# One transformer layer with product-key experts: all first expert products before the second ones, the second product with its operands exchanged, routing weights by accumulating scatters

## The chip, the cores and the metric

The kernel runs on one core of one Trainium2 chip. The metric is the device time of one execution in microseconds, the median of three runs. Five engines matter: PE (TensorE matmul, with PEld for its weight loads), DVE (VectorE), ACT (ScalarE), POOL (GpSimd, which also issues the indirect transfers) and SP (SyncE, which issues most loads). Matrix work is fp32: each operand is split in a high and a low half, and each 128-row block takes three products, hi·hi, hi·lo and lo·hi.

## The reference

256 prompt tokens and 64 sample tokens pass one layer of width 2048: attention in three branches, gates, an output product, and then a layer of 16,384 experts, which takes most of the time:

```python
s = jnp.einsum('thpc,hpkc->thpk', q, sub_keys)          # 8 heads, 2 halves, 128 keys
s1, i1 = lax.top_k(s[:, :, 0], 16); s2, i2 = lax.top_k(s[:, :, 1], 16)
cand_s = s1[..., :, None] + s2[..., None, :]
top_s, top_j = lax.top_k(cand_s.reshape(tb, 8, 256), 16)
eidx = take(i1 * 128 + i2, top_j); g = softmax(top_s)   # 128 experts per token
a = gelu(einsum('td,thkd->thk', xb, expert_u[eidx]))
return einsum('thk,thkd->td', g * a, expert_v[eidx])
```

## The kernel before, in words

One program holds all instructions; a planner with estimated clocks (`Plan`) writes out the order in which they stand on each engine. Weight matrices come as tiles of 512 KB ("halves"): SP loads `raw` (128x1024), ACT writes `hi`, DVE writes `lo` = raw - hi, and PE does the 24 matmuls of the half (`Stream`, L359; every other operation is recorded by one helper, L221). Each engine runs its instructions in order: a DVE instruction that waits holds up every `lo` behind it.

The first 1,129 us are the attention part and the query product. Then come the experts. For the 256 prompt tokens every expert is computed densely, in 32 groups of 4x128 experts:

- `Up(e)`: x times `pu`, two halves of 24 matmuls 128x256 (the tile is the stationary operand, 256 tokens move). ACT applies gelu and writes `hs`. Groups below `NSPILL` = 20 are written to memory (`hd`) and read back later.
- `weigh`: `hs` times the routing weights `gg` (zero for experts not chosen) gives `w`, split in hi and lo.
- `Down(q, c)`: `w` times `pv`, summed in PSUM over 8x128 experts, added by DVE to `x2` (the sum `r<-r,mm`, features by tokens). 256 tokens move.
- The order is 22 groups of Up (NSPILL + RES), then Up and Down alternately, then Down alone.

The routing weights G are built by `g_unit`, 64 units of four tokens: DVE makes one-hot tiles `ob` and `oa` of the chosen keys, POOL multiplies `ob` with the high and the low half of the weights (`wH`, `wL`), PE multiplies `oa` and `ob` (four matmuls `bk`), ACT and DVE put both halves together in `st`, and SP writes it to memory as `gd`, which is read back as `gg`.

The 64 sample tokens are not computed densely. For each of two tables (`pur`, `pvr`), 128 indirect gathers on POOL fetch 128 rows of 4 KB into one of four `gs` slots. DVE takes a product with a running sum of each `pur` tile (`dot`, form `gs<-gs,xs`), and adds each `pvr` tile times a weight to `x2s` (`axpy`). The next gather into a slot waits for the DVE instruction that reads it.

The few lines behind this that the steps below touch (`split_one` of the stream, `dot`, and the operands of Up and of Down, stationary or moving by their place):

```python
            act.activation(hi, raw, AF.Copy)
            dve.tensor_tensor(lo, raw, hi, op=ALU.subtract)
...
        plan.see(gs)
        yield
        dve.scalar_tensor_tensor(gs, gs, 1.0, R["xs"], op0=ALU.mult, op1=ALU.mult, accum_out=R["dots"][:, j:j + 1])
        X["GS"].give(gs)
...
            w, e = w_of[self.q], b % 8
            return self.ps[:, :DN], w[:, 0, e, :], w[:, 1, e, :], e == 0, e == 7
```

Of the kernel before, what the change touches and what calls it, by code (L numbers as in the profile page):

```python
# [33 lines left out]
RES = 2  # L34
NSPILL = 20
NGS = 4
HSN = 4
RATE = 380e3
GLAT = 5.0
# [3 lines left out]
TB = 16  # L43
LA = 5
SA = 3

# [34 lines left out]

class Task:
# [4 lines left out]
class Plan:  # L87
# [4 lines left out]
    def __init__(self):  # L92
        self.clk = {e: 0.0 for e in ("pe", "act", "dve", "pool", "dma")}
        self.task = self.main = Task(None)
        self.tasks = []
        self.done = {}
        self.uses = {}
        self.table = None

# [37 lines left out]
    def move(self, queue, out, src):  # L137

        at = max(self.last(out, True), self.last(src, False))
        if queue != "sync":  # L140
            at = self.clk[queue] = max(self.clk[queue], at) + (1.0 if queue == "pool" else 0.1)
        n = size(out) * out.shape[0] * 4
        self.clk["dma"] = max(self.clk["dma"], at) + n / RATE
        self.touch(out, self.clk["dma"] + 2.0, True)
        self.touch(src, self.clk["dma"] + 2.0, False)

    def gather(self, out, idx):
        at = self.clk["pool"] = max(self.clk["pool"], self.last(out, True), self.last(idx, False)) + 1.05
        self.clk["dma"] = max(self.clk["dma"], at) + size(out) * out.shape[0] * 4 / RATE
        self.touch(out, self.clk["dma"] + GLAT, True)  # L150

# [5 lines left out]
    def spawn(self, gen):  # L157
        self.tasks.append(Task(gen, self.task.at))
# [53 lines left out]
class Engine:  # L212
# [4 lines left out]
    def __getattr__(self, op):  # L217
        f = getattr(self.eng, op)

        def call(*a, **k):  # L220
# [4 lines left out]
            if op == "indirect_dma_start":  # L225
                p.gather(out, k["in_offset"].ap)
                return r
# [13 lines left out]
def pe_cost(op, a, k):  # L241
    n = size(a[2]) / (2.4e3 if op == "matmul" and a[2].dtype == F32R else 0.6e3)
    return max(0.107, n + 0.003) if op == "matmul" else 0.216
# [6 lines left out]
def dve_cost(op, a, k):  # L250
# [3 lines left out]
    return 0.07 + n / 0.96e3 * (6.2 if op == "reciprocal" else 1)  # L254
# [12 lines left out]
def hybrid_kernel(ctx: ExitStack, tc: tile.TileContext, ins, outs, stop=None):  # L267
# [20 lines left out]
    RAW = Slots(plan, stream, "raw", [128, 1024], F32, LA)  # L288
    HI = Slots(plan, stream, "hi", [128, 1024], F32R, SA + 1)
    LO = Slots(plan, stream, "lo", [128, 1024], F32R, SA + 1)  # L290
# [11 lines left out]
    pool.memset(one, 1.0)  # L302
    mhalf = consts.tile([128, 1], F32, name="mhalf")
# [5 lines left out]
    class Stream:  # L309
        def __init__(self):  # L310
            self.loads, self.halves = deque(), deque()

        def fetch(self):
            p, h = next(self.src, (None, 0))
            if p is None:
                return False
            raw = RAW.take()
            p.load(raw, h)
            self.loads.append((p, h, raw))
            return True  # L320

        def split_one(self):
            p, h, raw = self.loads.popleft()
            hi, lo = HI.take(), LO.take()
            act.activation(hi, raw, AF.Copy)
            dve.tensor_tensor(lo, raw, hi, op=ALU.subtract)
            RAW.give(raw)
            self.halves.append((p, h, hi, lo))

        def fill(self):  # L330
            while RAW.free and self.fetch():
                pass

        def ahead(self):
            self.fill()
            while HI.free and self.loads:
                if self.halves and plan.last(self.loads[0][2], False) > plan.now() + 1:
# [10 lines left out]
        def half(self):  # L348
            p, h, hi, lo = self.halves.popleft()
# [17 lines left out]
            HI.give(hi)  # L367
            LO.give(lo)

    eng = Stream()  # L370

    class Piece:

        GAP = 0.0025
# [135 lines left out]

    s1 = ExitStack()
# [24 lines left out]
    def late_consts():  # L536
# [17 lines left out]
        dve.tensor_scalar(bgh, vec[:, V_BG:V_BG + 48], 0.5, None, op0=ALU.mult)  # L554

# [442 lines left out]
    spawn(late_consts())  # L998

# [131 lines left out]
    def open_route():  # L1131
# [3 lines left out]
        R["x2s"], R["xs"] = (p.tile([128, W], F32, name=n) for n in ("x2s", "xs"))  # L1135
        p = open_pool(route, "route")
        for n in ("iT0", "iT1", "wH", "wL"):
            R[n] = p.tile([128, DN], F32R if n == "wH" else F32, name=n)
        for n in ("idx", "wS", "dots", "act"):
            R[n] = p.tile([128, 128], U32 if n == "idx" else F32, name=n)  # L1140
# [13 lines left out]
        spawn(rows_task())  # L1154
        for _ in range(LANES):
            spawn(route_lane())
        spawn(weights_lane())
# [19 lines left out]
    def rows_task():  # L1177

        x2s, xs = R["x2s"], R["xs"]
        for a in range(PARTS):  # L1180
            pool.dma_start(xs[a * S:a * S + S], ins["gffn"][a:a + 1].to_broadcast([S, W]))
        yield from need(("xb",))
        for k0 in range(0, KT, 4):
            bk, = yield from take(BK)
            a = k0 * 128 // W
            n, rows, c = S * a + S, slice(S * a, S * a + S), k0 * 128 % W
            for k in range(4):
                pe.transpose(bk[:n, k * 128:k * 128 + 128], x2[:, k0 + k, T - n:T], ident)
            yield
            act.activation(x2s[rows, c:c + 512], bk[rows, :], AF.Copy)  # L1190
            BK.give(bk)
# [5 lines left out]
        dve.scalar_tensor_tensor(xs, x2s, r2[:, 3:4], xs, op0=ALU.mult, op1=ALU.mult)  # L1197

# [4 lines left out]
    def wq_in(h, p):  # L1203
        def go(ps):
# [9 lines left out]
            if p == 1:  # L1214
                plan.see(sk)
                yield
                for i in range(3):
# [66 lines left out]
    def weights_lane():  # L1284
        yield from need(*[("dec", i) for i in range(3)])
        rtmp.close()
        q = open_pool(gtmp, "gtmp")
        OA = Slots(plan, q, "oa", [128, 4, 128], F32R, 3)
        OB = Slots(plan, q, "ob", [128, 4, 2, 128], F32R, 3)
        ST = Slots(plan, q, "st", [128, 128, TB], F32, 2)  # L1290
        st = None
        for t0 in range(0, DN, 4):
            if t0 % TB == 0:
                st, = yield from take(ST)
            oa, ob = yield from take(OA, OB)
            spawn(g_unit(t0, oa, ob, OA, OB, ST, st))
        while len(gdone) < DN // 4:
            yield
        gtmp.close()
        open_late()  # L1300
        mark("G")

    gdone = []
    gd = dram.tile([DN // TB, 128, 132 * TB], F32, name="gd")
    hd = dram.tile([NG, 128, GE * DN], F32, name="hd")

    def decode(i):
# [25 lines left out]
        for p in range(2):  # L1333
            for c in range(2):
# [5 lines left out]
                pool.tensor_tensor(b4, b4, R["ix"][:, i, hs, p, None, :].to_broadcast([128, 4, 16, 16]), op=ALU.mult)  # L1340
# [4 lines left out]
        rows = slice(0, 128) if i < 2 else slice(64, 64 + DN - TP)  # L1345
        n = rows.stop - rows.start
        if n:
            bk, = yield from take(BK)
            for a, nm in enumerate(("i0", "i1", "wt")):
                pe.transpose(bk[:, a * 128:a * 128 + n], R[nm][rows, i].rearrange("p h k -> p (h k)"), ident[rows, rows])  # L1350
            yield
            c = slice(i * 128, i * 128 + n)
            for a, nm in enumerate(("iT0", "iT1", "wH")):
                act.activation(R[nm][:, c], bk[:, a * 128:a * 128 + n], AF.Copy)
            dve.tensor_tensor(R["wL"][:, c], bk[:, 256:256 + n], R["wH"][:, c], op=ALU.subtract)
            BK.give(bk)
        if i == 2:
# [11 lines left out]
            dve.tensor_scalar(R["idx"], bk[:, 0:128], float(PARTS), cst[:, C_PART:C_PART + 1], op0=ALU.mult, op1=ALU.add)  # L1369
            act.activation(R["wS"], bk[:, 128:256], AF.Copy)  # L1370
# [10 lines left out]
    def g_unit(t0, oa, ob, OA, OB, ST, st):  # L1381

        io = cst[:, None, C_IO:C_IO + 128].to_broadcast([128, 4, 128])
        col = lambda nm: R[nm][:, t0:t0 + 4, None].to_broadcast([128, 4, 128])
        dve.tensor_tensor(ob[:, :, 1, :], io, col("iT1"), op=ALU.is_equal)
        pool.tensor_tensor(ob[:, :, 0, :], ob[:, :, 1, :], col("wH"), op=ALU.mult)
        pool.tensor_tensor(ob[:, :, 1, :], ob[:, :, 1, :], col("wL"), op=ALU.mult)
        dve.tensor_tensor(oa, io, col("iT0"), op=ALU.is_equal)
        yield
        b2 = yield from take(BK, BK)  # L1390
# [349 lines left out]
```

## Time and profile before

| | |
|---|---|
| median of three runs | 2735.09 us (2731.73 to 2736.88) |
| the profiled execution | 2734.69 us, its span 2732.9 us |
| PE busy | 2633.5 us, 96% of the span |
| DVE, ACT, POOL busy | 2024.8 (74%), 1137.6 (42%), 941.2 us (34%) |
| moved by DMA | 626.31 MB, mean 229 GB/s |
| mean granted clock of TensorE | 0.985 |

The span is what the profiler records from the first to the last instruction; the execution's own time is 1.8 us longer. Busy times are averages over stages that have different limits, so each stage is read by itself below.

### The profile page before, as it was taken

The page shows a single profiled execution, that of the slowest core. Times are in us where ns is not written, and L with a number is a line of the kernel's source. Part 1 is how long each engine was busy: PE and PEld are TensorE (multiplying, and loading weights), DVE is VectorE, ACT ScalarE, POOL GpSimd, SP SyncE. Part 2 cuts the span into 40 slices and gives each one's busy share as a digit, 9 for nine tenths or more (in the row PEclk, how much of TensorE's full clock was granted, in tenths as well). Part 3 has the DMA queues.
Part 4 walks back from the last instruction along what each step waited for, and adds up shares of the span by engine and source line. Part 5 has one row for each costly group of instructions (what it writes and reads, how often), then busy time and mean ns, then how long its engine had stood idle before and what let it go on. Part 6 is the DMA issues. An engine that isn't in the chain of part 4 may idle for free. (4 is left out here: it accounts for less than half of the span.)

```text
span 2732.9 us, 49761 instructions
## 1 busy us (share of the span) xinstructions
PE 2633.5 (96%) x19824; PEld 2587.2 (95%) x19824; DVE 2024.8 (74%) x3201; ACT 1137.6 (42%) x1613; POOL 941.2 (34%) x728
## 2 busy tenths in 40 slices
PE   7999999999999999999889898999999999999998
PEld 5899989999999999999889898999999999999997
DVE  8545666344444449999999998888778888888887
ACT  4344444333333334344444444444444444344442
POOL 7423342000001222045878877422223321122122
PEclk9999999999999999999999999999999999999999
DMA  7433333444444554456777787798988888888887
GB/s 229 166 124 120 123 113 131 150 151 147 154 147 147 176 173 141 152 185 222 271 279 275 272 284 271 296 318 302 333 310 308 310 329 298 310 299 312 289 293 255
DMA packets 217560, 626.31 MB, mean 229 GB/s; under 512 B 19824, under 2 KB 74096, under 8 KB 215280
## 3 DMA queue, kind: packets, MB, share of 16 engines
q1 hardware_dynamic: 174944, 470.40, 49.1%
q0 software_dynamic: 39504, 142.24, 14.9%
q10 hardware_dynamic: 2880, 10.49, 1.0%
q8 instruction: 157, 2.57, 0.4%
q14 instruction: 75, 0.61, 0.1%
HBM read 589.36 MB, written 33.69 MB: 228 GB/s over the span
## 5 line engine op out<-in xcount | busy, mean ns | idle before, releaser
L221 DVE TENSOR_TENSOR lo<-raw,hi 128x1024 fp32r<-128x1024 f32 x792 | 1035.7, 1311 | 568.3 <-ACT hi L221 560.8
L221 ACT ACTIVATE hi<-raw 128x1024 fp32r<-128x1024 f32 x792 | 835.0, 1058 | 1106.1 <-PE mm L359 961.0
L359 PE MATMUL mm<-xb,hi 128*128 128x256 f32 x4096 | 758.6, 287 | 2.9 <-ACT hs L221 2.8
L359 PE MATMUL mm<-w,hi 128*128 128x256 f32 x4096 | 737.6, 283 | 0.0
L359 PEld LDWEIGHTS mm<-xb,hi 128*128 128x128 f32 x4096 | 654.4, 196 | 3.3 <-ACT hs L221 3.0
L359 PEld LDWEIGHTS mm<-w,hi 128*128 128x128 f32 x4096 | 639.0, 192 | 0.0
L359 PE MATMUL mm<-x_g,hi 128*128 128x320 f32 x2688 | 602.9, 313 | 0.0
L359 PE MATMUL mm<-xb,lo 128*128 128x256 f32 x2048 | 587.9, 287 | 0.8 <-DVE lo L221 0.8
L359 PE MATMUL mm<-w,lo 128*128 128x256 f32 x2048 | 579.6, 283 | 0.0
L359 PEld LDWEIGHTS mm<-x_g,hi 128*128 128x128 f32 x2688 | 447.2, 188 | 8.0 <-issue 3.9
L359 PE MATMUL mm<-x_g,lo 128*128 128x320 f32 x1344 | 415.7, 309 | 0.9 <-DVE lo L221 0.9
L359 PEld LDWEIGHTS mm<-xb,lo 128*128 128x128 f32 x2048 | 402.2, 196 | 1.3 <-DVE lo L221 1.2
L359 PEld LDWEIGHTS mm<-w,lo 128*128 128x128 f32 x2048 | 393.2, 192 | 0.0
L221 POOL DMA_INDIRECT gs<-pvr,idx x128 | 178.6, 1395 | 531.3 <-DVE x2s L221 525.4
L221 POOL DMA_INDIRECT gs<-pur,idx x128 | 188.9, 1476 | 223.0 <-DVE gs L221 199.6
L359 PEld LDWEIGHTS mm<-x_g,lo 128*128 128x128 f32 x1344 | 252.7, 188 | 1.2 <-DVE lo L221 1.2
L221 POOL TENSOR_TENSOR r<-r 128x320 f32<-128x320 f32 (+2 forms) x39 | 39.6, 1017 | 403.0 <-DVE r L221 398.4
L221 DVE SCALAR_TENSOR_TENSOR gs<-gs,xs 128x1024 f32<-128x1024 f32 x128 | 173.1, 1355 | 0.1
L221 DVE SCALAR_TENSOR_TENSOR x2s<-gs,act,x2s 128x1024 f32<-128x1024 f32 x128 | 163.7, 1279 | 1.8 <-DMA gs<-pvr,idx 1.5
L221 POOL TENSOR_TENSOR ob<-ob,wL 128x512 fp32r<-128x512 f32 x64 | 142.3, 2223 | 5.0
L221 DVE TENSOR_TENSOR r<-r,mm 128x256 f32<-128x256 f32 x256 | 106.3, 415 | 43.5 <-PE mm L359 43.4
L221 POOL TENSOR_TENSOR ob<-ob,wH 128x512 fp32r<-128x512 f32 x64 | 114.8, 1794 | 62.2 <-DVE ob L221 56.7
(246 smaller groups left out, 2730.3 us busy)
## 6 DMA issues: line engine op xcount, KB each, us to landing
raw<-pu SPq DMA_DIRECT2D x256, 512.0 KB
raw<-pv SPq DMA_DIRECT2D x256, 512.0 KB
raw<-win SPq DMA_DIRECT2D x168, 512.0 KB
raw<-wbr SPq DMA_DIRECT2D x32, 512.0 KB
raw<-wout SPq DMA_DIRECT2D x32, 512.0 KB
raw<-wq SPq DMA_DIRECT2D x32, 512.0 KB
gd<-st SPq DMA_DIRECT2D x16, 1024.0 KB
gg<-gd SPq DMA_DIRECT2D x16, 1024.0 KB
```

The source lines that it names most:

```text
L221: r = f(*a, **k)
L359: nc.tensor.matmul(o, stays, moves, start=first, stop=last and n == len(products) - 1)
```

## The change

1. **Order.** NSPILL + RES becomes 28 + 4 = 32: all 256 halves of Up stand before the first Down. 28 groups of `hs` go through memory.
2. **Down turned.** A 128-token block of `w` is now the stationary operand and 512 columns of `pv` move: 3,072 matmuls 128x512 in place of 6,144 of 128x256. `pv` comes in 1 MB loads, in 2 KB pieces, that take two ring slots. The sum `x2t` is tokens by features; `turn()` transposes `x2` into it at the start and `home()` transposes it back at the end.
3. **Routing weights.** `g_unit` goes. `clear()` writes zeros to `gd` early, by 32 DMAs from ACT's queue (16.8 MB in all). `scatters()` then adds each chosen weight to its place: 256 indirect DMAs on POOL, each of 128 words of 4 bytes. The first scatter of a head's round waits for the 16 of the round before in the same half of `gd`.
4. **Sample tokens.** 64 gathers per table of 128 rows of 8 KB (1 MB each), into two and later three slots. While the scatters are issued, one gather stands behind every eight of them.
5. **Buffers.** Part of `xb` becomes room for `w`, `hi` and `lo` when Up ends, and `r1` holds two gather slots; the ring of raw tiles is one shorter at first and longer later. Twelve decode products go from POOL to DVE. The planner's costs change.

```diff
-RES = 2
-NSPILL = 20
-NGS = 4
+RES = 4
+NSPILL = 28
+NGS = 3
+NJ = 128 // PARTS
+GFIRST = 16
+PACE = 4
...
-LA = 5
+LA = 4
...
+        for q in range(NG // 2):
+            for g in gd:
+                act.dma_start(g[q].rearrange("p (a x) -> p a x", x=128), zeros[:, None, :].to_broadcast([128, 2 * GE, 128]))
...
+    def scatters():
+        yield from need(*[("ga", i) for i in range(DN // 128)])
+        for h in range(8):
+            for k in range(16):
+                for i in range(DN // 128):
+                    own = rounds.setdefault((h, i), [])
+                    j = 16 * h + k
+                    r = pool.indirect_dma_start(
+                        out=gd[i].rearrange("q p (x o) -> (q p x) o", o=1),
+                        out_offset=bass.IndirectOffsetOnAxis(ap=R["ga"][:, i, j:j + 1], axis=0),
+                        in_=R["gw"][:, i, j:j + 1], in_offset=None, compute_op=ALU.add)
+                    earlier = rounds[h - 1, i] if k == 0 and h else []
+                    after(r, earlier)
...
-                pool.tensor_tensor(b4, b4, R["ix"][:, i, hs, p, None, :].to_broadcast([128, 4, 16, 16]), op=ALU.mult)
+                dve.tensor_tensor(b4, b4, R["ix"][:, i, hs, p, None, :].to_broadcast([128, 4, 16, 16]), op=ALU.mult)
...
-    def g_unit(t0, oa, ob, OA, OB, ST, st):
...
-        pool.tensor_tensor(ob[:, :, 0, :], ob[:, :, 1, :], col("wH"), op=ALU.mult)
-        pool.tensor_tensor(ob[:, :, 1, :], ob[:, :, 1, :], col("wL"), op=ALU.mult)
...
-            for j in range(128):
+            for j in range(NJ):
+                while src == "pur" and j > GFIRST + pairs[0] // PACE:
+                    yield
...
+    def block(self, b, hi, lo):
+            w, e, t = w_of[self.q], b // 2, b % 2
+            wh, wl = (w[:, i, e, 128 * t:128 * t + 128] for i in range(2))
+            vh, vl = (x.rearrange("p (k e d) -> p e k d", k=4, e=GE)[:, e % GE] for x in (hi, lo))
+            return (self.sums[t].rearrange("p (k d) -> p k d", k=4), e == 2 * GE - 1,
+                    ((wh, vh, e == 0), (wh, vl, False), (wl, vh, False)))
...
-        for c in range(8):
+        for c in range(4):
             yield Down(q, c, last)
```

On PE before, in the middle of the first expert product, the `bk` matmuls of two units of routing weights stand among those of `Up` (`mm<-xb`):

```order
L359 MATMUL mm_17795<-xb,lo_17675 128x256
L221 MATMUL bk_17811<-ob_17573,oa_17572 128x256 x2
L221 MATMUL bk_17812<-ob_17573,oa_17572 128x256 x2
L359 MATMUL mm_17795<-xb,hi_17674 128x256 x2
L359 MATMUL mm_17795<-xb,lo_17675 128x256
```

On PE of the changed program, where the last `Up` ends and the first `Down` begins (`w` from `weigh`, `mm_18165` and `mm_18166` the sums of the two token blocks):

```order
L419 MATMUL mm_18079<-xb,hi 128x256 x2
L419 MATMUL mm_18079<-xb,lo 128x256
L419 MATMUL mm_18165<-hi,w_12571 128x512
L419 MATMUL mm_18165<-lo,w_12571 128x512
L419 MATMUL mm_18165<-hi,w_12571 128x512
L419 MATMUL mm_18166<-hi,w_12571 128x512
```

The `bk` matmuls are gone; the first Down, which needs `w` and so the routing weights, stands right behind the last Up with no other work between.

On POOL before, in the same stretch, gathers stand among the products that make `ob`:

```order
L221 DMA gs_15642<-pur,idx 128x1024
L221 TENSOR_TENSOR ob_15601<-ob_15601,wH 128x4x128
L221 TENSOR_TENSOR ob_15601<-ob_15601,wL 128x4x128
L221 DMA gs_15760<-pur,idx 128x1024
L221 TENSOR_TENSOR ob_15747<-ob_15747,wH 128x4x128
```

On POOL of the changed program, the same stretch (`gd_92` and `gd_93` are the two halves of the routing weights, `r_80` holds addresses and weights, and as an output it is a gather slot):

```order
L274 DMA gd_92<-r_80 2097152x1
L274 DMA gd_93<-r_80 2097152x1
L274 DMA gs<-pur,idx 128x2048
L274 DMA gd_92<-r_80 2097152x1
L274 DMA gd_93<-r_80 2097152x1
L274 DMA gd_92<-r_80 2097152x1
L274 DMA gd_93<-r_80 2097152x1
L274 DMA gd_92<-r_80 2097152x1
L274 DMA gd_93<-r_80 2097152x1
L274 DMA gd_92<-r_80 2097152x1
L274 DMA gd_93<-r_80 2097152x1
L274 DMA r_80<-pur,idx 128x2048
```

Products of POOL's own are replaced by issues of transfers alone; from the first scatter to the last there are 256 scatters and 41 gathers.

On DVE of the changed program, in the later part of Up, the `dot` of a gathered tile stands among the `lo` of the stream:

```order
L274 TENSOR_TENSOR lo<-raw,hi 128x1024
L274 SCALAR_TENSOR_TENSOR gs,dots<-gs,xs 128x2048
L274 TENSOR_TENSOR lo<-raw,hi 128x1024 x3
L274 TENSOR_TENSOR lo<-raw_10055,hi 128x1024 x2
L274 TENSOR_TENSOR lo<-raw,hi 128x1024
L274 SCALAR_TENSOR_TENSOR r_80,dots<-r_80,xs 128x2048
```

One dot, which waits for its gather, now stands before every five or six `lo`, in a queue that runs in order.

## Rows read from the trace of the kernel before

**Rows 1.** The page: the span, then busy time, share of the span and instructions of each engine.

```profile
span 2732.9 us, 49761 instructions
PE 2633.5 (96%) x19824; PEld 2587.2 (95%) x19824; DVE 2024.8 (74%) x3201; ACT 1137.6 (42%) x1613; POOL 941.2 (34%) x728
```

**Rows 2.** Busy time by stage: start and end, length, then busy us (and instructions) of PE, PEld, DVE, ACT and POOL, the granted TensorE clock, DMA share and GB/s. The stages are: ahead of the experts; the first halves of Up while the routing still runs; the building of G beside Up; the rest of Up and Down; the end.

```profile
0.00:1129.06 1129.06, 1095.06 (x7257) 1055.91 (x7258) 646.50 (x1292) 446.18 (x703) 271.76 (x315) 0.99 0.44 149
1129.06:1274.30 145.24, 140.32 (x1145) 139.84 (x1144) 133.87 (x300) 65.52 (x86) 51.81 (x35) 0.98 0.58 193
1274.30:1738.00 463.70, 417.69 (x3262) 411.65 (x3261) 439.12 (x518) 213.89 (x315) 375.74 (x197) 0.94 0.76 271
1738.00:2719.30 981.30, 980.44 (x8167) 979.85 (x8165) 798.54 (x1088) 411.98 (x509) 240.03 (x181) 1.00 0.87 309
2719.30:2732.90 13.60, 0.03 (x1) 0.00 (x0) 6.76 (x6) 0.00 (x0) 1.87 (x1) 0.69 0.30 108
```

**Rows 3.** The same view of the matmuls of the stream alone (`mm`) in 500 us of Up and Down (no POOL column), and of all work on the tile `bk` (the routing weights' matmuls) while G is built.

```profile
2000.00:2500.00 500.00, 500.00 (x4167) 499.85 (x4166) 58.12 (x140) 5.77 (x16) 1.00 0.87 311
...
1274.30:1738.00 463.70, 48.00 (x256) 37.98 (x256) 71.49 (x126) 68.96 (x128) 0.94 0.76 271
```

**Rows 4.** Waits while G is built (1274.3 to 1738): who waited for whom, us in total, times, longest.

```profile
POOL ob L221 <- DVE ob L221: 56.7, 20, 5.5
PEld bk L221 <- POOL ob L221: 33.6, 10, 5.1
PE bk L221 <- POOL ob L221: 31.4, 10, 4.9
...
PE bk L221 <- DVE st L221: 14.2, 10, 3.8
```

**Rows 5.** Timeline of PE: start, duration, instruction. First two matmuls 128x512 that are 50 steps apart, at the start of the program, then four transposes and the matmul behind them.

```profile
33.20 0.39 PE L359 MATMUL mm<-lo,x_m 128*128 128x512 f32 x1
...
44.87 0.39 PE L359 MATMUL bk<-hi,x_m 128*128 128x512 f32 x1
...
1085.09 0.60 PE L221 MATMUL bk<-cst,r 128*64 128x128 f32 x4
1085.44 0.54 PE L359 MATMUL mm<-x2g,hi 128*128 128x320 f32 x2
```

**Rows 6.** Groups of instructions by form: count, busy us, mean ns of one, idle time before them and what ended it.

```profile
L221 DVE TENSOR_TENSOR lo<-raw,hi 128x1024 fp32r<-128x1024 f32 x792 | 1035.7, 1311 | 568.3 <-ACT hi L221 560.8 <-PE bk L221 1.9
L221 ACT ACTIVATE hi<-raw 128x1024 fp32r<-128x1024 f32 x792 | 835.0, 1058 | 1106.1 <-PE mm L359 961.0 <-issue 65.7 <-DMA raw<-pv 24.5
L221 POOL DMA_INDIRECT gs<-pur,idx x128 | 188.9, 1476 | 223.0 <-DVE gs L221 199.6 <-issue 9.0 <-DVE idx L221 7.6
L221 POOL DMA_INDIRECT gs<-pvr,idx x128 | 178.6, 1395 | 531.3 <-DVE x2s L221 525.4 <-DVE lo L221 3.4 <-issue 2.1
L221 DVE SCALAR_TENSOR_TENSOR gs<-gs,xs 128x1024 f32<-128x1024 f32 x128 | 173.1, 1355 | 0.1
L221 POOL TENSOR_TENSOR ob<-ob,wL 128x512 fp32r<-128x512 f32 x64 | 142.3, 2223 | 5.0
L221 DVE TENSOR_TENSOR big<-xt,cst 128x1024 f32<-128x1024 f32 x12 | 14.4, 1203 | 0.0
```

**Rows 7.** Timeline of POOL: gathers that follow one another directly while G is built, then gathers of the second table at their longest and their shortest; and of DVE beside the first of those.

```profile
1345.99 1.83 POOL L221 DMA_INDIRECT gs<-pur,idx  x1 [0.30 <-DVE st L221]
1348.12 1.98 POOL L221 DMA_INDIRECT gs<-pur,idx  x1 [0.30 <-issue]
...
2105.28 2.02 POOL L221 DMA_INDIRECT gs<-pvr,idx  x1 [10.53 <-DVE x2s L221]
2121.11 0.95 POOL L221 DMA_INDIRECT gs<-pvr,idx  x1 [5.84 <-DVE x2s L221]
...
2105.25 1.22 DVE L221 TENSOR_TENSOR lo<-raw,hi 128x1024 fp32r<-128x1024 f32 x1
2106.39 1.28 DVE L221 SCALAR_TENSOR_TENSOR x2s<-gs,act,x2s 128x1024 f32<-128x1024 f32 x1
```

**Rows 8.** DMA queues: packets, MB, share of the 16 engines. First the total and the two large queues in 2000 to 2500, then the large queue in the first 60 us.

```profile
DMA packets 56784, 155.29 MB, mean 311 GB/s; under 512 B 4588, under 2 KB 21047, under 8 KB 56736
q1 hardware_dynamic: 44064, 108.48, 60.6%
q0 software_dynamic: 12672, 46.14, 25.8%
...
q1 hardware_dynamic: 19376, 14.21, 80.0%
```

**Rows 9.** ACT and DMA early in the program by the view of rows 2, and ACT's queue at one spill of `hs`.

```profile
137.00:683.00 546.00, 541.01 (x3636) 517.52 (x3635) 290.55 (x528) 220.47 (x417) 122.70 (x144) 1.00 0.38 133
...
1154.84 0.34 ACTq L221 DMA_DIRECT2D hd<-hs  x1
```

**Rows 10.** The end of the program: DVE's last instructions and SP's last issue.

```profile
2719.36 0.42 DVE L221 TENSOR_TENSOR r<-r,mm 128x256 f32<-128x256 f32 x1 [2.46 <-PE mm L359]
2726.49 1.28 DVE L221 SCALAR_TENSOR_TENSOR x2s<-gs,act,x2s 128x1024 f32<-128x1024 f32 x1 [1.55 <-DMA gs<-pvr,idx]
...
2727.80 0.33 SPq L221 DMA_DIRECT2D ys<-x2s  x1
```

More of the change, by code (lines that the diff above doesn't have):

```diff
@@ L225, in call @@
             if op == "indirect_dma_start":
[L226 removed]
+                if k["in_offset"] is None:
+                    p.scatter(k["out_offset"].ap, k["in_"])
+                else:
+                    p.gather(out, k["in_offset"].ap)
                 return r
@@ L335, in ahead @@
             self.fill()
-            while HI.free and self.loads:
-                if self.halves and plan.last(self.loads[0][2], False) > plan.now() + 1:
+            while self.loads and HI.left() >= self.loads[0][0].SLOTS:
+                if self.halves and max(plan.last(self.loads[0][2], False), plan.clk["dve"] - AHEAD) > plan.now() + 1:
                     break
@@ L508, in row_norm @@
         yield
+    gd = [dram.tile([NG // 2, 128, 2 * GE * 128], F32, name=f"gd{i}") for i in range(DN // 128)]
     s1 = ExitStack()
@@ L554, in late_consts, with clear @@
         dve.tensor_scalar(bgh, vec[:, V_BG:V_BG + 48], 0.5, None, op0=ALU.mult)
+    def clear():
+        yield from need(("x",))
+        for q in range(NG // 2):
+            for g in gd:
+                act.dma_start(g[q].rearrange("p (a x) -> p a x", x=128), zeros[:, None, :].to_broadcast([128, 2 * GE, 128]))
+            at = plan.now() + 12.0
+            while plan.now() < at:
+                yield
     def x_scales():
@@ new lines, in hybrid_kernel, with turn, home @@
+    x2t = []
+    def turn():
+        yield from need(("rows",))
+        for t in range(DN // 128):
+            for k0 in range(0, KT, 4):
+                bk, = yield from take(BK)
+                for k in range(4):
+                    pe.transpose(bk[:, k * 128:k * 128 + 128], x2[:, k0 + k, 128 * t:128 * t + 128], ident)
+                yield
+                act.activation(x2t[0][:, t, 128 * k0:128 * k0 + 512], bk, AF.Copy)
+                BK.give(bk)
+        mark("turned")
+    def home(c):
+        y, = yield from take(X["HS"])
+        yield
+        for t in range(DN // 128):
+            bk, = yield from take(BK)
+            for k in range(4):
+                pe.transpose(bk[:, k * 128:k * 128 + 128], x2t[0][:, t, (4 * c + k) * 128:(4 * c + k) * 128 + 128], ident)
+            yield
+            act.activation(y[:, :, 128 * t:128 * t + 128], bk.rearrange("p (k t) -> p k t", k=4), AF.Copy)
+            BK.give(bk)
+        sync.dma_start(outs["yT"][4 * c:4 * c + 4].rearrange("k d t -> d k t"), y)
+        X["HS"].give(y)
@@ L1575, in down @@
     def down(q, last=False):
-        for c in range(8):
+        for c in range(4):
             yield Down(q, c, last)
```

338 lines of the change are left out of this document (197 added, 141 removed).

## The prediction

> **What bounds the kernel now.** I read the page's busy times first, then the busy times by stage, then the waits of the one stage where PE is not full, then single durations.
>
> PE is busy 96% of a span of 2732.9 us [rows 1], so the kernel is bound by matmuls nearly everywhere, and only two things can move it: fewer or cheaper PE steps, and the places where PE stands idle. By stage [rows 2]: from 1738 to 2719 us PE is busy for 980.4 of 981.3 us, nothing to gain but the steps themselves. From 1274 to 1738 it is busy for 417.7 of 463.7 us only; here G is built beside Up, DVE is busy for 439 us (95%) and POOL for 376 us (81%). In that stage the routing matmuls `bk` wait for `ob` from POOL (33.6 us before the weight load, 31.4 us before the matmul, which overlap) and for `st` on DVE (14.2 us), and POOL waits for `ob` from DVE (56.7 us) [rows 4]. So it is a ring DVE, POOL, PE, DVE in which the two elementwise engines are nearly full, and PE stops since its queue is in order. That stage and the count of the steps are what the change touches.
>
> Prices. A step of 128x256 takes 500/4167 = 0.120 us [rows 3]. A step of 128x512 takes (44.87 - 33.20)/50 = 0.2333 us [rows 5]: 50 steps of the same fp32 halves, early in the program. Four transposes take 1085.44 - 1085.09 = 0.35 us [rows 5].
>
> **The change part by part,** against the profiled execution's own 2734.7 us (the median of the runs shown is 0.4 us above it).
>
> *G's matmuls go.* 256 `bk` steps [rows 3] by 0.120 = 30.7 us less.
>
> *G's stall goes.* In the order 2,994 Up matmuls lie between the first and the last `bk` matmul. At 0.120 they need 359.3 us, the `bk` 30.7; the stage took 463.7. The rest, 73.7 us, is stall and slowed steps (the granted clock is 0.94 there): 73.7 us less, if nothing takes its place.
>
> *Down turned.* 6,144 x 0.120 = 737.3 becomes 3,072 x 0.2333 = 716.7: 20.6 us less. By the Trainium skill, page "TensorE: Matmul & The Clock Gate", section "Back-to-back issue gap", an isolated step takes N/2.4 + 2.5 ns, 109 and 216 ns for these widths; the turn would then give 670.9 - 663.0 = 8 us, and the sum would be 2682. The rows show 120 and 233; they decide.
>
> *Transposes and fold.* `turn()` and `home()` are eight groups of four transposes each, and the sample rows take four groups more than before: 20 x 0.35 = 7 us, and four fold matmuls of 512 columns: 8.5 us more.
>
> *DVE at the start of Up.* The first 145 us [rows 2] lose 145.2 - 1145 x 0.12 = 7.8 us with DVE at 92%. The 12 decode products that leave POOL come to DVE (1.20 us each by a like form [rows 6], 14 us), and six dots of the wider form (at most twice 1.355 - some 2.3 us, 14 us) stand before the last address. This routing part ends at about Up's half 73, near 205 us. Some of the 28 us meets a full DVE: 10 us more; 0 if it fits the idle 8%, 28 if none does.
>
> *POOL's train.* From half 73 to Up's end are 183 halves of 24 x 0.120 = 2.88 us, 527 us. In it POOL must issue 256 scatters and 41 gathers, and only then can `weigh` have G. No accumulating scatter is in the trace. The nearest row is the gather: mean 1.476 and 1.395 us [rows 6], 0.30 us between two that follow directly [rows 7]. At 1.436 + 0.30 = 1.74 us the train is 297 x 1.74 = 516 us. Seven rounds wait for the landing of the round before; some 3 us each (estimate), 537 in all: 10 us late. From below: at the shortest, 0.95 us, it is 297 x 1.25 = 371, hidden. From above: at 2.02 us, 297 x 2.32 = 689, with the round waits 710, 183 us late. I take the mean, for the durations vary with what DVE does beside them, and DVE is less full here than when G is built.
>
> *Where a late scatter shows.* One dot stands before every five or six `lo` and waits for a gather that stands behind eight scatters. DVE's queue is in order: if POOL falls behind, `lo` falls behind, and PE after it. So lateness appears spread over Up, not as one gap, and there is no buffer that would take it.
>
> *From Up to Down.* The first Down stands directly behind the last Up. Last scatter landed, `gg` (1 MB) read, `hs` times `gg`, ACT's copy, DVE's second half for two groups: products of 128x1024 take 1.31 and copies 1.06 us [rows 6], so one group is 3.7 us, two with dots between them 10; with some 3 us for landing and 5 us for the load it is 18 us, of which a few are ahead of the last Up: 15 us more. With G in time it is 0.
>
> *DMA in Down.* Before, DMA moves 311 GB/s at a share of 0.87 [rows 3], which is 357 GB/s at a full share. Of Down's 128 halves (5.6 us each, 1.05 MB) the 96 in which the 64 second gathers (1.05 MB each) stand carry 100.7 + 67.1 MB, and spilled `hs` and `gg` some 23.6: 191.4 MB in 537.6 us are 356 GB/s, right at that ceiling. The first 20 halves carry 44.8 MB in 112 us, 400 GB/s: 13.5 us late. With 8 us for the rest (0 at 357, 14 at 347 GB/s) it is 22 us more; 0 if the second slot and the longer ring take up the peaks.
>
> *End.* Before, 13.6 us pass after the last sum [rows 2, 10], with the last gathers' axpys and the store of `ys`. Now the last axpy stands six halves ahead of the end; what is left is a transpose, a copy and a store: about 7.8 us, 6 less.
>
> *At nothing.* `clear`'s 32 issues of 0.34 us are 11 us of an ACT that is 40% busy, and its 16.8 MB meet a DMA share of 0.38 [rows 9]. 128 fewer gather issues, one raw tile less in the attention part (DMA share 0.44 [rows 2]), eight more spills: beside PE. Without that cover the 11 us would be the price.
>
> Sum: -30.7 - 73.7 - 20.6 + 8.5 + 10 + 10 + 15 + 22 - 6 = -65.5: **2669 us**.
>
> **The rivals.**
>
> *R1, the scatters bind and the kernel gets slower.* POOL's train at a pitch p costs 297 x (p - 1.74) more, so the gain of 65.5 us is gone at p = 1.96. At 2.1 us (the gathers that follow one another while G is built are 2.13 apart [rows 7]) it is 107 us more, 2776; at 2.32, 2.02 plus the gap, 172 more, 2841. For it: those gathers had DVE's `lo` beside them, and so will most scatters. Against: the long gather of 2.02 us began with `lo`, and an axpy that also reads two SBUF operands began while it ran and took its usual 1.28 us; the short ones of 0.95 us [rows 7] show what is left without it. By the Trainium skill, page "SBUF — State Buffer", section "SBUF: two separate sides", a DVE operation with two SBUF inputs and a GpSimd operation that reads SBUF shut each other out for a whole instruction; `lo` and dot together fill some 57% of Up, and 0.95/0.43 + 0.3 would make 2.5 us, deep in this rival. The axpy that ran beside the gather speaks against it in this form. Chance 0.10.
>
> *R2, everything stays hidden.* Scatters issue at 1.6 us or less, DMA takes its peaks, the changeover costs little: the 57 us of losses shrink to 10 or 20, 2612 to 2640. For it: POOL has 0.95 us gathers, and `hd`, `gg` and gathers need not come in time to the microsecond. Chance 0.18.
>
> *R3, the descriptors bind.* 32,768 words of 4 bytes are as many transfers. In the 527 us the loads of `pu` (95.9 MB), 41 gathers (43.0) and spills (10.5) need 283 GB/s, 0.79 of 357. What is left, 0.21 x 527 x 16 engines, gives each word 54 ns. A packet of 733 bytes takes 0.80 x 60 x 16/19376 = 39.6 ns [rows 8], so they fit; an accumulation that reads and then writes could take twice that, 79 ns, and cost 51 us, 2720. From 86 ns on the kernel is slower. Chance of that 0.06. The Trainium skill, page "DMA: Bandwidth & Descriptors", section "Specifications", says that below 512 bytes a transfer becomes a read and a write, which speaks for this one; no row here shows a 4-byte transfer.
>
> *R4, part of the cost but not all:* scatters at 1.8 to 1.95 us, or words of 60 to 85 ns: 2700 to 2729. Chance 0.14.
>
> *R5, the turn gives nothing:* if the 512-wide step with `w` stationary takes 0.240, Down stays at 737 and the time is 2690, inside the forecast's own range.
>
> **How the numbers follow.** A difference under 0.2% can't be told from no change here: 2729.6 to 2740.6. The forecast, 2640 to 2700, has 0.48; R2 0.18; R4 0.14; R1 0.10; R3's slower end 0.06; no change by accident 0.04. Faster is 0.48 + 0.18 + 0.14 = 0.80, slower 0.16. The range goes from R2's lower end, 2612, to 2750, which leaves out most of R1, the far part of R3 and little of R2, under 2 in 10.
>
> **What would show it.** Up: PE busy 97% or more between its first and last matmul, with a length of 737 + 20 us; if it is longer, waits of PE for `lo` and of DVE for the gather behind scatters (R1), or a DMA share near 1 (R3). Scatters: duration and pitch on POOL's timeline, 1.44 and 1.74. Down: steps 0.233 apart, DMA share above 0.95 in the first 110 us. Changeover: one gap of about 15 us before the first matmul 128x512. The end: 8 us after the last matmul. The forecast is wrong if the pitch leaves 1.5 to 1.95, or if Up's loss has another cause than POOL.

## The result, and the profile after

The changed kernel takes 2748.5 us (median of four runs, 2747.2 to 2752.9) against 2733.4 for the kernel before on the same chips: a ratio of 1.0059, 95% interval 1.004 to 1.0078. It is slower by 0.6%, where 2669 us, faster than before, was forecast. The profiled execution took 2748.4 us.

The page of the changed kernel, to be read beside [rows 1]:

```profile
span 2746.4 us, 41010 instructions
PE 2596.4 (95%) x16576; PEld 2413.2 (88%) x16576; DVE 1756.0 (64%) x2331; ACT 1047.3 (38%) x1281; POOL 975.5 (36%) x717
```

PE has 37 us less work and DVE 269 us less, and yet the span grew. So the gain that the change made on PE came back as idle time. The busy times by stage, cut where Up starts, where the first scatter is issued, where Up ends, where Down starts and ends (columns as in [rows 2]):

```profile
1128.30:1338.50 210.20, 210.20 (x1763) 210.20 (x1763) 188.55 (x461) 100.31 (x131) 28.23 (x32) 1.00 0.66 233
1338.50:1955.40 616.90, 564.00 (x4486) 559.27 (x4485) 313.37 (x270) 220.89 (x275) 521.93 (x285) 0.96 0.83 245
1955.40:1999.50 44.10, 0.12 (x2) 0.00 (x0) 14.17 (x11) 5.25 (x5) 28.32 (x18) 0.56 0.74 243
1999.50:2740.30 740.80, 725.67 (x3104) 587.30 (x3104) 605.69 (x406) 276.78 (x171) 137.86 (x77) 0.98 0.86 323
2740.30:2746.40 6.10, 1.42 (x9) 0.83 (x8) 0.83 (x2) 1.20 (x2) 0.00 (x0) 0.94 0.25 86
```

4,486 steps of 0.120 us are 538 us; they took 617. Then PE stands still for 44 us. In both stretches POOL is the busy one: 522 of 617 us (85%), against 51% for DVE and 36% for ACT. The scatters on POOL (least, median and longest duration in ns, first and last start):

```profile
L274 POOL DMA_INDIRECT gd<-r x256: 1548/1576/3561, 1338.5 to 1980.7; - x128
```

Their mean is 491.8/256 = 1.92 us. With the 41 gathers among them and 0.30 us between two, POOL's train lasts from 1338.5 to 1982.2, 643.8 us or 2.17 us for each of its 297 instructions. POOL stands idle in it for no more than these 0.30 us, but for some 9 us at the starts of rounds. The chain that ended last runs through its end (start, length, what):

```profile
1978.83 1.55 POOL gd L274
...
1980.69 3.79 DMA gd<-r
...
1984.55 9.88 DMA gg<-gd
...
1994.52 1.23 DVE hs L274
1995.74 2.21 DVE r L274 x2
1997.95 1.15 DVE w L274
...
1999.56 12.48 PE mm L419 x42
```

The last scatter, its landing, the load of the routing weights, the weighing of one group with dots between, the first matmul of Down: 17.3 us from the last scatter's end to PE. So Down begins where POOL's train ends, plus 17 us.

### The profile page after: what moved, and what is told of

Same layout as the page of the kernel before. It is cut to its first block, busy times and chain, and to the rows that moved or that the text cites. A ratio compares the mean times of both kernels' runs of the same rounds, so it can differ in the third digit from the quotient of the medians.

```text
span 2746.4 us, 41010 instructions
## 1 busy us (share of the span) xinstructions
PE 2596.4 (95%) x16576; PEld 2413.2 (88%) x16576; DVE 1756.0 (64%) x2331; ACT 1047.3 (38%) x1281; POOL 975.5 (36%) x717
## 5 line engine op out<-in xcount | busy, mean ns | idle before, releaser
L274 DVE TENSOR_TENSOR lo<-raw,hi 128x1024 fp32r<-128x1024 f32 (+1 forms) x622 | 866.5, 1407 | 548.8 <-ACT hi L274 542.7
L274 ACT ACTIVATE hi<-raw 128x1024 fp32r<-128x1024 f32 (+1 forms) x622 | 732.2, 1178 | 1192.5 <-PE mm L419 902.6
L274 POOL DMA_INDIRECT gd<-r x256 | 491.8, 1921 | 86.4 <-issue 74.7
L419 PE MATMUL mm<-hi,w 128*128 128x512 f32 x688 | 223.2, 400 | 44.0 <-ACT hs L274 44.0
L419 PE MATMUL mm<-hi,xb 128*128 128x512 f32 x688 | 220.3, 394 | 0.0
L419 PEld LDWEIGHTS mm<-hi,w 128*128 128x128 f32 x688 | 131.3, 191 | 76.0 <-ACT hs L274 44.2
L419 PEld LDWEIGHTS mm<-hi,xb 128*128 128x128 f32 x688 | 130.0, 189 | 27.9 <-issue 1.0
L419 PE MATMUL mm<-lo,w 128*128 128x512 f32 x344 | 137.9, 401 | 3.2 <-DVE lo L274 3.2
L419 PE MATMUL mm<-lo,xb 128*128 128x512 f32 x344 | 134.8, 392 | 2.2 <-DVE lo L274 2.2
L419 PE MATMUL mm<-xb,w 128*128 128x512 f32 x504 | 126.0, 406 | 9.5 <-DVE xb L274 9.1
```

The source lines that it names most:

```text
L274: r = f(*a, **k)
L419: nc.tensor.matmul(o, stays, moves, start=first, stop=last and n == len(products) - 1)
```

## The experiments

Theory A: POOL's train sets when Down begins, and it is long because a scatter takes longer than the price in the sum. What makes it longer was open between two accounts: DVE's work beside it holds it, or the scatter itself costs more. Rival C: DMA, wider gathers or dots in DVE's queue slow Up, whatever the scatters do. In the table, times are of the profiled execution; the columns "first scatter", "last scatter" and "Down" hold starts, the last that of Down's first matmul. The kernels that leave something out (e2, e7, e11, e12) have one run each.

| kernel | scatter mean us | first scatter | last scatter | Down | time us |
|---|---|---|---|---|---|
| changed | 1.92 | 1338.5 | 1980.7 | 1999.6 | 2748.4 |
| e1 lo in another form | 1.90 | 1337.2 | 1978.4 | 1997.7 | 2745.1 |
| e2 no scatters | - | - | - | 1897.8 | 2644.6 |
| e6 lo in four pieces | 1.98 | 1337.8 | 2000.4 | 2019.8 | 2767.9 |
| e7 lo on ACT | 1.73 | 1337.7 | 1928.8 | 1947.3 | 2696.3 |
| e8 e6, dots in two | 1.87 | 1334.8 | 1966.2 | 1984.9 | 2726.9 |
| e13 early start | 1.94 | 1300.6 | 1963.7 | 1995.3 | 2750.8 |
| e10 e13, dots in two | 1.84 | 1303.3 | 1935.9 | 1967.3 | 2709.0 |
| e9 e8, early start | 1.77 | 1302.7 | 1912.1 | 1942.5 | 2683.3 |
| e14 e9, first head written | 1.69 | 1303.2 | 1894.6 | 1925.7 | 2667.6 |
| e12 all scatters written | 1.25 | 1337.9 | 1843.4 | 1895.8 | 2640.8 |

From the first matmul of Down to the end it is 741 to 756 us in every row. So the time follows Down's start, and Down's start follows the last scatter (18 to 20 us behind that scatter's start where the train starts late, 30 to 32 where it starts early), until the train ends before Up does, as in e12.

**e2: without scatters.**

```diff
-                    r = pool.indirect_dma_start(
-                        out=gd[i].rearrange("q p (x o) -> (q p x) o", o=1),
...
+                    plan.scatter(R["ga"][:, i, j:j + 1], R["gw"][:, i, j:j + 1])
```

> The changed kernel with the 256 scatters left out (the routing weights stay zero), the order of all else as it was planned with them. Theory A (POOL's train of scatters ends last, and sets when Down begins): Up takes 210 + 538 us instead of 827, Down begins a few us behind it, the time is 2748 - 123 to - 105, 2625 to 2645. Theory C (the wider gathers, the dots in DVE's queue or DMA slow Up, whatever the scatters do): Up stays over 790 us and the time over 2700.

Measured: 2644.6 us. By stage, as above:

```profile
1129.00:1339.00 210.00, 210.00 (x1761) 210.00 (x1761) 188.36 (x463) 99.95 (x130) 27.91 (x31) 1.00 0.66 233
1339.00:1877.90 538.90, 538.90 (x4492) 538.74 (x4490) 318.46 (x272) 221.29 (x276) 72.81 (x44) 1.00 0.79 287
1877.90:1897.80 19.90, 0.05 (x1) 0.00 (x0) 13.95 (x11) 5.16 (x5) 5.01 (x3) 0.57 0.88 339
1897.80:2636.80 739.00, 723.30 (x3104) 585.37 (x3104) 605.26 (x406) 276.74 (x170) 134.72 (x77) 0.99 0.87 324
```

With the same order of everything else, PE is full for all of Up, and 104 us are gone: 78 of them in Up, 24 in the gap. Rival C falls. Wider gathers, dots in the in-order queue and a DMA share of 0.79 hold up nothing by themselves; the scatters' price is 104 us, and without it the changed kernel would be 90 us faster than the kernel before. Whether it is paid on POOL or in the transfers, e2 alone does not tell.

**e1 and e5: lo by another instruction.** In the trace of the changed kernel the scatters come in two kinds: 1.55 to 1.58 us where no DVE instruction with two SBUF operands ran at their start, and up to 3.56 us where one did. I first took this for a property of the `tensor_tensor` form, in which `lo` is written.

```diff
-            dve.tensor_tensor(lo, raw, hi, op=ALU.subtract)
+            dve.scalar_tensor_tensor(lo, raw, 1.0, hi, op0=ALU.mult, op1=ALU.subtract)
```

> The changed kernel with one edit: DVE writes lo as a scalar_tensor_tensor (raw times 1.0 minus hi) in place of a tensor_tensor; values, order and DVE time nearly the same. Theory A (a scatter is held while a tensor_tensor with two SBUF operands runs on DVE; a scalar_tensor_tensor such as the dot does not hold it): scatters fall from a mean of 1.92 us to the 1.56 us they have with nothing or a dot beside them, POOL's train from 644 to 256 x 1.87 + 41 x 1.3 + 11 = 543 us, about what the rest of Up needs (538), so the time is 2748 - 100 = 2648, at most 2670. Theory B (the scatter's length comes from its own transfers or from the software queue, and lo only happens to run then): mean stays at 1.85 or more, 2735 to 2755.

Measured: 2748.25 us (2743.8 to 2755.5), scatters' mean 1.90. The time is what Theory B expected, but the two kinds of scatters are there as before, so it is not B's reason. The edit did not tell the two apart: the form was the wrong variable.

> The kernel before with the same edit as e1: lo by scalar_tensor_tensor. Theory A: POOL's products for ob (means 1.79 and 2.22 us) and the gathers are no longer held by lo, nor lo by them, so the ring DVE, POOL, PE in the stage of G turns faster and gives back 20 to 50 of its 74 us: 2685 to 2715. If that stage is bound by DVE's own 95% instead, nothing changes: 2730 to 2740.

Measured: 2732.0 us, ratio 1.000 (0.9985 to 1.0015). No change here either; POOL's products for `ob` take 2.15 and 1.83 us, about as long as before.

Laid side by side, POOL's and DVE's timelines of the changed kernel show what holds a scatter (start, duration, instruction):

```profile
1508.94 1.55 POOL L274 DMA_INDIRECT gd<-r  x1 [0.30 <-issue]
1510.79 1.89 POOL L274 DMA_INDIRECT gd<-r  x1 [0.30 <-issue]
1512.99 1.98 POOL L274 DMA_INDIRECT gd<-r  x1 [0.30 <-issue]
1515.27 1.97 POOL L274 DMA_INDIRECT gd<-r  x1 [0.30 <-issue]
1517.54 1.55 POOL L274 DMA_INDIRECT gd<-r  x1 [0.30 <-issue]
...
1508.91 2.35 DVE L274 SCALAR_TENSOR_TENSOR gs<-gs,xs 128x2048 f32<-128x2048 f32 x1 [3.59 <-DMA gs<-pur,idx]
...
1511.19 4.62 DVE L274 TENSOR_TENSOR lo<-raw,hi 128x1024 fp32r<-128x1024 f32 x4
```

The scatter of 1510.79 begins in a dot that ends at 1511.26; 1.42 us later, at 1512.68, it is done. The one of 1512.99 begins in the second `lo`, which ends at 1513.54, and is done at 1514.97, 1.43 later. The first, which began within 0.03 us of the dot's own start, and the last, which began as a `lo` ended, take 1.55. So it is one rule for dots and `lo`: a scatter that starts while a DVE instruction with two SBUF operands runs waits for that instruction's end and then needs 1.43 us, and never takes less than 1.55. Worked out for each of the 256 scatters from the ends of the single DVE instructions, the rule meets the measured duration within 0.11 us every time. By it, 85 scatters waited some 50 us in all for `lo`, 36 waited 43 us for dots (the expectations below put these at 49 us, and at 38 scatters).

**e7: lo off DVE.**

```diff
+            if hasattr(p, "e") and plan.has(("ga", 0), ("ga", 1)):
+                act.activation(lo, raw, AF.Copy)
+            else:
+                dve.tensor_tensor(lo, raw, hi, op=ALU.subtract)
```

> The changed kernel; while the scatters run, the lo of Up's tiles is a copy of raw written by ACT (so the values of Up are not the reference's), and DVE has dots alone. Theory A2: the 49 us that scatters wait for lo go, the 43 us for dots stay: scatters' mean 1.73, train 595 us, the time 2699, range 2690 to 2715. Theory B: mean 1.85 or more, 2735 or more. If ACT, busy for some 2.4 of each 2.88 us now, holds up Up, PE waits for lo from ACT and Up ends later, but Down's start stays where the train ends.

Measured: 2696.3 us, mean 1.73, waits for `lo` 2 us and for dots 42. The train ends 52 us earlier and the time is 52 us less. That DVE's `lo` hold scatters is shown by this, not only argued; for the dots e8 and e10 show it. Up ended at 1876 and PE then waited 71 us for the train: the stall only moved from within Up to behind it.

**e6 and e8: shorter pieces.**

```diff
+            cut = 4 if p.SLOTS == 1 and plan.has(("ga", 0), ("ga", 1)) else 1
+            for x in range(cut):
+                c = slice(1024 * p.SLOTS // cut * x, 1024 * p.SLOTS // cut * (x + 1))
+                dve.tensor_tensor(lo[:, c], raw[:, c], hi[:, c], op=ALU.subtract)
```

> The changed kernel; while the scatters run, each lo of 128x1024 is written by four tensor_tensors of 128x256. Theory A2, formed from the traces of the changed kernel and of e1 (a scatter that starts while a two-operand DVE operation runs waits for that one operation's end and then needs 1.43 us; if none runs it takes 1.55): 85 scatters wait 49 us in all for lo, 38 wait 43 us for dots. Pieces a quarter as long leave some 9 of the 49 us: POOL's train 644 - 40 = 604 us, the time 2748 - 40 = 2708, range 2700 to 2720. Theory B (the scatter's own transfers): no change, since bytes and DVE's share are the same or a little larger: 2740 to 2760.

Measured: 2769.3 us, 61 more than expected and slower than the changed kernel. The rule of "that one operation's end" does not hold for short pieces; 24 of e6's 256 scatters were held past the piece in which they began, one of them so (POOL and DVE of e6):

```profile
1589.30 4.39 POOL L274 DMA_INDIRECT gd<-r  x1 [0.30 <-issue]
...
1585.48 6.79 DVE L274 TENSOR_TENSOR lo<-raw,hi 128x256 fp32r<-128x256 f32 x20
```

Twenty pieces of 128x256 ran from 1585.48 to 1592.27 without a break; the scatter got through none of the eight boundaries behind its start and ended 1.42 us after the last piece. At the end of a dot or of a 128x1024 `lo` it does get through although the next `lo` follows without a gap, as the scatters of 1510.79 and 1512.99 show. Where between 256 and 1024 elements that changes was not tried.

```diff
+        for x in range(2):
+            c = slice(1024 * x, 1024 * x + 1024)
+            dve.scalar_tensor_tensor(gs[:, c], gs[:, c], 1.0, R["xs"][:, c], op0=ALU.mult, op1=ALU.mult,
+                                     accum_out=R["dots"][:, NJ * x + j:NJ * x + j + 1])
```

> e6 with each dot of 128x2048 in two pieces of 1024. Theory A2: of the 43 us that scatters wait for dots about 20 stay: train 644 - 63 = 581, the time 2748 - 63 = 2685, range 2672 to 2700, under the kernel before. Theory B: 2740 to 2765.

Measured: 2726.9 us, ratio to before 0.997 (0.996 to 0.999). Against e6 the halved dots give 42 us, where 23 were expected: the waits for dots fall from 47 to 21 us, 26 us, Down starts 35 us earlier, and Down itself is 6 us shorter. What makes up the rest wasn't followed.

**e13, e10, e9: an earlier start.** Scatters of the first half start once its own addresses stand; a small memset separates two scatters of one half.

```diff
-        yield from need(*[("ga", i) for i in range(DN // 128)])
+        yield from need(("ga", 0))
...
+            if before == 0 and plan.has(("ga", 1)) and count[1] < 128:
+                i = 1
+            elif count[0] < 128:
+                i = 0
...
+            if i == before:
+                pool.memset(R["pad"], 0.0)
```

> e8, and the scatters of the first half of the routing weights begin when its addresses stand (1302 in the changed kernel's trace), not when those of both halves do (1338); a tiny memset on POOL stands between two scatters of the same half. The train starts up to 37 us earlier, and some 20 scatters of one half alone at each end cost a memset each, some 0.4 us: a gain of 15 to 30 us over e8, 2655 to 2672. If the train's start doesn't matter, the time of e8.

> The changed kernel with the dots in two pieces of 1024 and the early scatters of e9, but each lo whole (128x1024). e6 against the changed kernel says that quartered lo cost 21 us, since a scatter that meets a run of short pieces is held for several of them; then without them e9's 2688 becomes 2667, range 2650 to 2690. If the quartered lo were harmless in this order (scatters waited 33 us for lo in e9, 60 in e6), the time is that of e9 or up to 20 us more.

> The changed kernel with the early start of the scatters alone (e10 with dots whole). The train starts 36 us earlier, at 1302; two times some 18 scatters in a row of one half cost a memset each, about 0.9 us: 12 to 20 us of the 36 stay, against e10 the dots' waits come back (43 in place of 27 us): 2722, range 2712 to 2735.

Measured: e13 2749.6 us (no gain, 2722 expected), e10 2704.7, e9 2687.9 (2674 to 2702; ratio to before 0.984, 0.979 to 0.989). e9 gains 39 us on e8, more than the 15 to 30 expected, but as e8 itself came out 42 us late, e9 still lies above its range. Alone, the start 38 us earlier is lost again: the train is 21 us longer (its 30 memsets take 19.2 us), Down starts 32 us behind the last scatter's start instead of 19, and from there to the end it is 7 us longer. In SP's queue, which issues in order, the load of the routing weights stands behind six loads of `pv` whose ring slots come free as Up ends; it is issued 7.5 us after the last scatter's start, where the changed kernel issues it 1.3 us after, 6 MB of `pv` are ahead of it, and it takes 19.3 us where it took 9.9 (SP of e13):

```profile
1942.61 28.20 SPq L274 DMA_DIRECT2D raw<-pv  x6
1971.17 1.98 SPq L274 DMA_DIRECT2D gg<-gd  x4
```

The halved dots give 45 us here too (e13 to e10). Quartered `lo` cost 21 us with the late start (e6 against the changed kernel) and gave 17 with the early one (e9 against e10); the scatters' waits for `lo` in these four kernels, e6, changed, e9 and e10, were some 60, 50, 33 and 47 us. So the sign is not fixed; that it depends on where runs of pieces fall is likely but not shown, and I had expected the wrong one for e10.

**e12 and e14: written instead of added.** What the rule leaves is the 1.55 us of a scatter that nothing holds.

```diff
-                        in_=R["gw"][:, i, j:j + 1], in_offset=None, compute_op=ALU.add)
+                        in_=R["gw"][:, i, j:j + 1], in_offset=None)
```

> The changed kernel with scatters that write their words instead of adding them (an expert chosen by two heads of a token keeps one of its weights, so the prompt rows differ a little from the reference's). The prediction took the gathers' mean, 0.95 us alone plus waits, for a scatter; the trace shows 1.55 us alone. If the addition makes the 0.6 us, a scatter alone takes 0.95 to 1.05, the train falls from 644 by some 150 us to 490, under the 538 us that Up needs, and the time to 2650, give or take 15. If 128 words written from SBUF cost 1.55 in any case, scatter and time stay: 1.5 us or more alone, 2740 to 2755.

Measured: 2640.8 us. Duration, first and last start:

```profile
L274 POOL DMA_INDIRECT gd<-r x256: 965/982/3032, 1337.9 to 1843.4; - x128
```

Alone a scatter that writes takes 0.97 us, as long as a gather; the addition costs 0.58 us on POOL for 128 words; what POOL does in that time no row shows. The train ends 31 us before Up, and the time is about that without scatters.

```diff
-                in_=R["gw"][:, i, j:j + 1], in_offset=None, compute_op=ALU.add)
+                in_=R["gw"][:, i, j:j + 1], in_offset=None, compute_op=ALU.add if h else ALU.bypass)
```

> e9 with the 32 scatters of the first head written instead of added (a token's 16 experts of one head are distinct and the words were cleared, so the sum is the same). If the addition's 0.58 us on POOL is paid per scatter, 32 x 0.58 = 18 us leave the train and the time is 2688 - 18 = 2670, range 2655 to 2685; if the train's end no longer decides, because the loads of gg and of the first tiles of pv behind it do, the time stays at 2680 to 2690.

Measured: 2674.3 us (2667.6 to 2679.6), ratio to before 0.979 (0.977 to 0.982), 13.6 less than e9, where 18 were expected; the two kernels' runs overlap, but in the profiled ones the train is 18 us shorter. It is the fastest of the kernels that leave nothing out, 74 us under the changed kernel and 57 under the kernel before.

**e11: Down without the second gathers.**

```diff
-            for j in range(NJ):
+            n = NJ if src == "pur" else 2
+            for j in range(n):
```

> The changed kernel with two of the 64 gathers and axpys of the second table, so that 65 MB less are moved beside Down (the sample rows are not the reference's). If DMA near its ceiling makes Down's idle time (15 of 741 us, behind late tiles of pv), Down falls to 717 + 6 (half clock after the gap) + 3 (transposes) = 726 and the time to 2734. If DVE's order makes it, Down stays within 4 us of 741 and the time within 4 of 2748.

Measured: 2723.9 us; Down takes 720.5 us instead of 740.8, less than the 726 expected (columns as in [rows 2]):

```profile
1999.50:2720.00 720.50, 717.25 (x3112) 583.60 (x3112) 474.80 (x345) 277.71 (x173) 22.34 (x15) 1.00 0.67 243
```

The second gathers and their axpys together cost 20 us of Down and 4 us behind it. PE's idle time falls from 15 to 3 us; the rest is granted clock (1.00 for 0.98). The run takes away DMA's load and DVE's work at once, so it does not tell the two accounts apart. The trace of the changed kernel does so in part. One of PE's longest stops in Down (PE, ACT and DVE; here `xb` holds `hi` and `lo`):

```profile
2288.01 2.32 PE L419 MATMUL mm<-xb,w 128*128 128x512 f32 x5 [4.23 <-DVE xb L274]
...
2281.33 1.89 ACT L274 ACTIVATE xb<-raw 128x2048 fp32r<-128x2048 f32 x1
...
2282.81 2.35 DVE L274 SCALAR_TENSOR_TENSOR x2s<-r,act,x2s 128x2048 f32<-128x2048 f32 x1
2285.07 0.68 DVE L274 TENSOR_TENSOR x2t<-x2t,mm 128x512 f32<-128x512 f32 x1
2285.67 2.29 DVE L274 TENSOR_TENSOR xb<-raw,xb 128x2048 fp32r<-128x2048 f32 x1
```

The tile had come and its `hi` was written at 2283.22, but an axpy and a sum stood ahead of the `lo` on DVE. It is so in the stops of 2152.2, 2283.8 and 2560.5 us, 11.3 of the 15.1 us; the one of 2312.2 (2.8 us) follows a late tile of `pv`. ACT's waits for `pv` fall from 118 to 5 us in e11, so DMA may have used up the lead before those stops; that was not tested.

## Why the prediction was wrong

**The step that failed is the price of a scatter**, "At 1.436 + 0.30 = 1.74 us the train is 297 x 1.74 = 516 us". Measured: 643.8 us, against 537 with the round waits. The 256 scatters took 1.92 in place of 1.436 us, 124 us more; the gathers (1.30 us each, not 1.436) and the round waits (9 us in all, not 21) together 17 us less. The mean of the gathers holds two parts, 0.95 us alone and 0.49 us of waiting. The waits of scatters were smaller, 0.37 us (30 us less in all). But the part alone is 1.55, not 0.95 (154 us more), and e12 shows that this is the addition. The pitch came to 2.17, outside the 1.5 to 1.95 that the prediction allowed. No row of before had an accumulating transfer; I bounded it by gathers, and the upper bound, 2.02, was a gather that waits and not an unheld scatter. A new kind of instruction wants a price for its own part and one for its waits; a mean over another kind holds neither.

**The reading of the hold was wrong too.** I argued that the axpy which ran beside a 2.02 us gather spoke against a hold. What it shows is only that a gather that has got through does not hold DVE back. That gather began in a `lo` (2105.25, 1.22 us) that ended at 2106.47, 1.19 us after the gather's start. By the rule of the scatters, 0.12 us less than its 0.95 are left from there: 1.19 + 0.83 = 2.02, as measured [rows 7]. The rule of the Trainium skill that I cited there, page "SBUF — State Buffer", section "SBUF: two separate sides", agrees with the traces where POOL comes second: a scatter waits for the DVE instruction that runs. In the other direction no wait is seen: dots took 2.29 us with scatters and 2.28 in e2, and of the `lo` of 128x1024 in the train the 144 that began while a scatter ran took 1.22 us each, like the other 44.

**The other steps.**
- *G's matmuls and stall go:* right. Without scatters (e2) Up runs full, 538.9 us for 4,492 steps.
- *Down turned:* right. In steady state the step is 0.233 us, and Down's 740.8 us are 716.7 + 24.1; 22 for DMA and 3 for transposes were forecast.
- *DMA in Down:* right in size, 20 us by e11, but the cause is not shown: DVE's order makes most of the stops as far as the trace goes, and how much of the 20 us is DMA stays open. Part of it is not idle time but granted clock.
- *DVE at the start of Up:* 10 us forecast. The 210.2 us hold 1,661 steps (199 us) and transposes (6 us); 5 us were lost, less than before.
- *From Up to Down:* 15 us forecast for a train that ends 10 us late. The chain took 17.3 us, and that it came so near is in part luck: the 3 us for a landing and 5 us for the load had no row, the load took 9.9 us, and one group was weighed ahead of Down (5 us), not two (10 us). The gap is 44 us, since 27 us of the train's lateness stand there.
- *Where a late scatter shows:* half right. 53 us stood in Up as PE's waits for `lo` behind dots, the rest in one gap, for gathers run ahead of the last scatters. As e7 shows, this distribution doesn't matter: either way Down starts 17 us after the train.
- *At nothing:* right as far as seen. The stretch ahead of the experts takes 1128.3 us, 0.8 less.
- *End:* 6.1 us after Down, 7.8 forecast.
- *Transposes and fold:* 20 x 0.35 and four steps of 0.2333 make 7.9 us, not 8.5; it changes nothing.

**The rivals.** R1 came true, at a pitch of 2.17. Its price, 127 us, would be 2796; the time is 48 less, for the round waits were counted beside the pitch (about 20), Up's start lost 13 less, Up had 538 and not 527 us for the train, and the last 4 us are spread over the changeover, Down and the end. Its chance, 0.10, was too small: the point from which it decides, 1.96 us, lay 0.22 over a price that had no row of its own. R3 did not decide: in 1400 to 1950 the words took some 46 ns of one DMA engine each, where 39.6 was the estimate and 54 the limit, and DMA's share was 0.82. This comes from the software queue's share in that stretch, less 103 us for 36.83 MB at the 357 GB/s of before, for the 28,416 words of 222 scatters:

```profile
q0 software_dynamic: 37064, 36.83, 33.6%
```

R2's low price of a scatter came about only in e12, where nothing is added: 1.25 us and 2641, at the upper end of R2. R5 did not come: the step is 0.233 us.

## What to carry to other kernels

When a chain of small transfers is issued by one engine, price one of them alone and its waits apart, and count the whole train against the work that is to hide it: here 0.58 us more on each of 256 instructions cost 108 us (e12), with PE, DVE and DMA not full; the engine that issues them had no gap left beyond 0.30 us. Where such a transfer shares a time with vector work on two SBUF operands, its length depends on what runs at its start. Halving the dots to 1024 elements paid twice (42 and 45 us); cutting `lo` to 256 elements did not pay reliably, and a run of those let nothing through. A saving counts only up to the next thing in line: 38 us of earlier start were worth nothing alone, since they went into memsets and a load that stood behind others.

## What the runs showed of the hardware

- An indirect transfer of 128 words that adds takes POOL 1.55 us with nothing beside it, one that writes 0.97 us, and a gather of 128 rows 0.95 us, of 4 or 8 KB alike (4 KB in [rows 7]; 8 KB rows took from 0.94 us in e9).
- A DVE instruction with two SBUF operands that is under way when such a transfer starts holds it until its end. A sum with one operand in PSUM (`x2t<-x2t,mm`) does not: gathers that began in one took 0.94 us in the changed kernel. Back-to-back instructions of 1024 elements let it in between two; a run of twenty of 256 elements held one for 4.39 us.
- After the gap of 44 us, in which PE was busy for 0.12 us, TensorE ran at the lower of its two clock levels, 1.2 GHz (granted clock 0.50 from 1999.5 to 2003.0): 0.43 us for each step of 512 columns. From some 6 us on it ran at 2.4 GHz (1.00 from 2005.5 to 2010.0), 0.233 us a step (PE of the changed kernel):

```profile
2000.15 0.63 PE L419 MATMUL mm<-lo,w 128*128 128x512 f32 x1
2000.58 1.05 PE L419 MATMUL mm<-hi,w 128*128 128x512 f32 x2
...
2007.22 0.40 PE L419 MATMUL mm<-lo,w 128*128 128x512 f32 x1
2007.45 0.63 PE L419 MATMUL mm<-hi,w 128*128 128x512 f32 x2
```
